# An 8 KB copy from DRAM to DRAM on a second DMA queue, issued at the start of an elementwise multiply-GELU kernel

**Chip, cores, metric.** One core of one Trainium2 chip. The metric is device time in microseconds (us), the median of several executions.

## The reference

```python
x, y: (1024, 4096) float32
z = x * y
out = 0.5 * z * (1 + tanh(sqrt(2 / pi) * (z + 0.044715 * z**3)))   # float32
```

Two inputs of 16.8 MB are read and one output of 16.8 MB is written, 50.33 MB in all, with two elementwise passes between.

## The kernel before

Each of the 128 partitions owns one contiguous stretch of 32768 floats of x, y and the output. SP is the sequencer of SyncE and ACT that of ScalarE; what a queue has for one of the 16 DMA engines is called its ring there. All transfers are issued by SP, so all sit on one queue: x in two halves, y in a half and two quarters, the output in two halves. VectorE multiplies in place and ScalarE applies GELU in place, in tiles of 4096 floats per partition.

```python
X_LOADS = [(0, 16384), (16384, 32768)]
Y_LOADS = [(0, 16384, 0), (16384, 24576, 0), (24576, 32768, 8192)]
STEP = 4096
STORES = [(0, 16384), (16384, 32768)]
# ...
    _hoist(nc, [load_x(0).ins, load_y(0).ins])   # placed ahead of SP's first drain, before the opening barrier
    load_x(1)
    for i in (1, 2):
        nc.sync.wait_ge(sem_mul, (Y_LOADS[i][1] - Y_LOADS[1][0]) // STEP)
        load_y(i)
# ... VectorE multiplies, ScalarE applies GELU, in tiles of STEP ...
    for i, (a, b) in enumerate(STORES):
        nc.sync.wait_ge(sem_act, b // STEP)
        nc.sync.dma_start(out=out_r[:, a:b], in_=xs[:, a:b]).then_inc(sem_o[i], 16)
```

Of the kernel before, what the change touches and what calls it, by code (L numbers as in the profile page):

```python
# [1 line left out]

# [4 lines left out]


F32 = mybir.dt.float32
GELU = mybir.ActivationFunctionType.Gelu_apprx_tanh  # L10
# [7 lines that stand above are left out]
Y_RING = 16384  # L18


def _hoist(nc, issued):

    here = nc.cur_bb.bb.instructions
    first = nc.main_func.blocks[0].instructions
    for ins in issued:
        del here[next(k for k, i in enumerate(here) if i is ins or i.name == ins.name)]
    engine = issued[0].engine
    at = next(
        k
        for k, i in enumerate(first)  # L30
        if i.engine == engine and type(i).__name__ == "InstDrain"
    )
    first[at:at] = issued


@with_exitstack
def kernel(
    ctx: ExitStack,
    tc: tile.TileContext,
    x: bass.AP,  # L40
    y: bass.AP,
    out: bass.AP,
):
    nc = tc.nc
    P = nc.NUM_PARTITIONS

    x_r = x.flatten_outer_dims().rearrange("(p a) c -> p (a c)", p=P)
    y_r = y.flatten_outer_dims().rearrange("(p a) c -> p (a c)", p=P)
    out_r = out.flatten_outer_dims().rearrange("(p a) c -> p (a c)", p=P)
    total_f = x_r.shape[1]  # L50


    tc.close()
    tc.compile()  # L54

    xs = nc.alloc_sbuf_tensor("xs", [P, total_f], F32).ap()
    ys = nc.alloc_sbuf_tensor("ys", [P, Y_RING], F32).ap()
    sem_x = [nc.alloc_semaphore(f"sem_x{i}") for i in range(len(X_LOADS))]
    sem_y = [nc.alloc_semaphore(f"sem_y{i}") for i in range(len(Y_LOADS))]
    sem_o = [nc.alloc_semaphore(f"sem_o{i}") for i in range(len(STORES))]  # L60
    sem_mul = nc.alloc_semaphore("sem_mul")
    sem_act = nc.alloc_semaphore("sem_act")

    def load_x(i):
        a, b = X_LOADS[i]
        return nc.sync.dma_start(out=xs[:, a:b], in_=x_r[:, a:b]).then_inc(sem_x[i], 16)  # L66

    def load_y(i):
        a, b, r = Y_LOADS[i]
        return nc.sync.dma_start(  # L70
            out=ys[:, r : r + b - a], in_=y_r[:, a:b]
        ).then_inc(sem_y[i], 16)

    _hoist(nc, [load_x(0).ins, load_y(0).ins])
    load_x(1)
    for i in (1, 2):
        nc.sync.wait_ge(sem_mul, (Y_LOADS[i][1] - Y_LOADS[1][0]) // STEP)
        load_y(i)

    n = 0  # L80
    for i, (a, b, r) in enumerate(Y_LOADS):
        for j, (xa, xb) in enumerate(X_LOADS):
            if xa <= a < xb:
                nc.vector.wait_ge(sem_x[j], 16)
        nc.vector.wait_ge(sem_y[i], 16)  # L85
        for c in range(a, b, STEP):
            nc.vector.tensor_mul(  # L87
                out=xs[:, c : c + STEP],
                in0=xs[:, c : c + STEP],
                in1=ys[:, r + c - a : r + c - a + STEP],  # L90
            ).then_inc(sem_mul, 1)
            n += 1
            nc.scalar.wait_ge(sem_mul, n)
            nc.scalar.activation(  # L94
                out=xs[:, c : c + STEP], in_=xs[:, c : c + STEP], func=GELU
            ).then_inc(sem_act, 1)

    for i, (a, b) in enumerate(STORES):
        nc.sync.wait_ge(sem_act, b // STEP)
        nc.sync.dma_start(out=out_r[:, a:b], in_=xs[:, a:b]).then_inc(sem_o[i], 16)  # L100
    for i in range(len(STORES)):
        nc.sync.wait_ge(sem_o[i], 16)
    nums = sorted(s.num for s in [*sem_x, *sem_y, *sem_o, sem_mul, sem_act])
    assert nums == list(range(nums[0], nums[-1] + 1))
    nc.sync.sem_clear(range(nums[0], nums[-1] + 1))


# [1 line left out]
_INS = ['x', 'y']  # L109
_OUTS = [((1024, 4096), 'float32')]  # L110


# [23 lines left out]
```

## Time and profile before

| | before |
|---|---|
| median time, 4 runs | 120.81 us (120.68 to 120.92) |
| span in the profile | 119.5 us |
| VectorE, ScalarE busy | 29%, 25% |
| DMA engines busy | 98.5% |
| rate over the span | 421 GB/s |

How to read it: the kernel moves data, and the compute engines wait. The end comes when the last of the 16 DMA engines has written its last row. Each transfer of 128 partition rows is split so that every engine gets 8 rows, and the trace has a record of each row. What a change can win or lose is in the few microseconds at the start, at the turn from loads to stores, and in any packet added. The prediction adds this up and shows the lines.

### The profile page before, as it was taken

The numbers are of one execution on the slowest core, as the hardware profiler recorded it, in microseconds if no ns is written. First come the engines' busy times: TensorE is split into PE (matmuls) and PEld (weight loads), VectorE is DVE, ScalarE is ACT, GpSimd is POOL, SyncE is SP. The second block draws the span as 40 slices with busy tenths as digits, with TensorE's granted clock in tenths as the row PEclk, the third lists the DMA queues.
The fourth block names the chain that finished last, engine by engine and source line by source line (L and its number), as shares of the span: only waits on it lengthen the run. The fifth ranks groups of instructions, "written<-read, shape, count | busy, mean of one in ns | idle before, by whom it ended". The sixth has DMA issues, their size and how long they took to land.

```text
span 119.5 us, 68 instructions
## 1 busy us (share of the span) xinstructions
DVE 35.0 (29%) x8; ACT 30.2 (25%) x9; POOL 0.2 (0%) x4
## 2 busy tenths in 40 slices
DVE  0000000000000199999600049959990000000000
ACT  3000000000000006797780000977479200000000
POOL 0000000000000000000000000000000000000000
DMA  9889888998899889988898989998899888988890
GB/s 351 351 373 680 351 351 351 636 417 351 351 636 417 351 351 526 526 351 351 351 526 351 504 373 482 395 526 351 351 395 658 351 351 351 702 351 351 351 680 22
DMA packets 1008, 50.33 MB, mean 421 GB/s; under 512 B 112, under 2 KB 112, under 8 KB 112
## 3 DMA queue, kind: packets, MB, share of 16 engines
q1 hardware_dynamic: 1008, 50.33, 98.5%
HBM read 33.55 MB, written 16.78 MB: 421 GB/s over the span
## 4 chain that ended last, share of the span: by engine, by line
DMA 53%; DVE 22%; ACT 3%; SPq 0%; issue 0%; DVEq 0%
DMA ys<-in_y_dram 53%; DVE xs L87 22%; ACT xs L94 3%; SPq L66 0%; DVEq L85 0%
## 5 line engine op out<-in xcount | busy, mean ns | idle before, releaser
L87 DVE TENSOR_TENSOR xs<-xs,ys 128x4096 f32<-128x4096 f32 x8 | 35.0, 4421 | 54.7 <-DMA ys<-in_y_dram 54.7
L94 ACT ACTIVATE xs<-xs 128x4096 f32<-128x4096 f32 x8 | 28.9, 3617 | 61.1 <-DVE xs L87 61.1
L94 ACT ACT_TABLE_LOAD x1 | 1.3, 1283 | 1.9 <-PEq L54 1.9
L120 POOL MEMSET const-bfloat16-1.0<- 128x1 bf16 x1 | 0.1, 102 | 0.0
L120 POOL MEMSET const-uint8-127<- 128x1 uint8 x1 | 0.1, 102 | 0.0
L120 POOL MEMSET const-float32-1.0<- 128x1 f32 x1 | 0.1, 99 | 0.0
L120 POOL MEMSET const-float32-0.0<- 128x1 f32 x1 | 0.1, 98 | 0.2 <-issue 0.2
## 6 DMA issues: line engine op xcount, KB each, us to landing
ys<-in_y_dram SPq DMA_DIRECT2D x2, 4096.0 KB, 21.1
xs<-in_x_dram SPq DMA_DIRECT2D x2, 40.3
out_dram<-xs SPq DMA_DIRECT2D x2, 31.9
ys<-in_y_dram SPq DMA_DIRECT2D x1, 40.8
```

The lines of the kernel that those rows point to most:

```text
L87: nc.vector.tensor_mul(out=xs[:, c : c + STEP], in0=xs[:, c : c + STEP], in1=ys[:, r + c - a : r + c - a + STEP],).then_inc(sem_mul, 1)
L94: nc.scalar.activation(out=xs[:, c : c + STEP], in_=xs[:, c : c + STEP], func=GELU).then_inc(sem_act, 1)
L120: nc = _bacc.Bacc("TRN2", target_bir_lowering=False, num_devices=1)
```

## The change

The intent, as the short description has it, is a first transfer on ACT's queue: 64 B per partition are copied from x to the head of each partition's stretch of the output, which the first store overwrites later. Why one would want it isn't stated; the likely hope is that a tiny transfer takes a start-up cost off the large one. To keep the result right, SP waits for its semaphore ahead of the first store.

```diff
+    sem_w = nc.alloc_semaphore("sem_w")
@@
+    first = nc.scalar.dma_start(out=out_r[:, :16], in_=x_r[:, :16])
+    first.then_inc(sem_w, 16)
+    _hoist(nc, [first.ins])
     _hoist(nc, [load_x(0).ins, load_y(0).ins])
@@
+    nc.sync.wait_ge(sem_w, 16)
     for i, (a, b) in enumerate(STORES):
@@
-    nums = sorted(s.num for s in [*sem_x, *sem_y, *sem_o, sem_mul, sem_act])
+    nums = sorted(s.num for s in [*sem_x, *sem_y, *sem_o, sem_w, sem_mul, sem_act])
```

## The prediction

> **What bounds the kernel now.** I read four views, from coarse to fine. First the top of the page: which engine is busy, and how full the DMA engines are.
>
> ```profile
> DVE 35.0 (29%) x8; ACT 30.2 (25%) x9; POOL 0.2 (0%) x4
> ...
> DMA  9889888998899889988898989998899888988890
> ...
> DMA packets 1008, 50.33 MB, mean 421 GB/s; under 512 B 112, under 2 KB 112, under 8 KB 112
> ...
> q1 hardware_dynamic: 1008, 50.33, 98.5%
> ```
>
> The reader is to see that no compute engine is busy a third of the span, while the 16 DMA engines have work for 98.5% of it, without a hole in the row of digits. All transfers sit on one queue. The 1008 packets are 7 transfers x 16 engines x (8 rows + 1 semaphore write).
>
> Second, the chain that ended last, in order of time:
>
> ```profile
> 0.00 0.39 SPq L66
> 0.39 0.05 issue
> 0.44 40.80 DMA ys<-in_y_dram
> ...
> 58.80 21.99 DMA ys<-in_y_dram
> ...
> 80.88 8.77 DVE xs L87 x2
> 89.66 0.02 issue
> 89.68 3.62 ACT xs L94
> ```
>
> It passes through the loads and the last multiply and GELU, and stops there: the last store, issued at 93.3, isn't in it. It mustn't be read as "22% DVE on the path". The waits of the DMA queue's issuer and the issue table say what the end is:
>
> ```profile
> SPq L102 <- DMA out_dram<-xs: 25.8, 1, 25.8
> ...
> out_dram<-xs SPq DMA_DIRECT2D x2, 31.9
> ```
>
> The issuer waits 25.8 us for the last store, and that store is slow to land because the first store is still in front of it on the same engines (the two took 37.7 and 26.1 us from issue to landing). So the end is set by how much the 16 engines have to move in all and by when they start, not by any issue time in between.
>
> Third, the busy time in stretches (a packet is booked in the stretch where it starts; columns are stretch, length, DVE, ACT, POOL, clock, DMA share, GB/s):
>
> ```profile
> 0.00:1.00 1.00, 0.00 (x0) 0.00 (x0) 0.20 (x4) 1.00 0.00 0
> 1.00:2.00 1.00, 0.00 (x0) 0.07 (x1) 0.00 (x0) 1.00 3.13 1049
> 2.00:4.00 2.00, 0.00 (x0) 1.21 (x1) 0.00 (x0) 1.00 0.00 0
> 4.00:6.00 2.00, 0.00 (x0) 0.00 (x0) 0.00 (x0) 1.00 1.21 524
> 6.00:59.00 53.00, 17.43 (x4) 11.05 (x4) 0.00 (x0) 1.00 1.01 435
> ```
>
> Nothing moves in the first microsecond. Between 1 and 2 us every engine starts its first 64 KiB row, and the share of 3.13 in a stretch of 1 us says that these rows take 3.13 us each. The next rows start between 4 and 6 us: 2 x 1.21 = 2.42 us each. So the first row of each engine is 0.71 us longer than a later one. That is the start-up cost that this change might aim at.
>
> The single DMA packet records of the trace bear it out: a 64 KiB row takes 2.418 us in steady state and 2.63 to 3.29 us as an engine's first; first packets start at 1.01 to 1.70 us; the engines end at 118.60 to 119.07 us. From them the whole time adds up. Each engine moves 50.33 MB / 16 = 48 rows of 64 KiB, 48 x 2.418 = 116.06. The last engine to finish starts at 1.68, adds 0.55 in its first row and 0.74 in two rows of 32 KiB near 77 us, where loads give way to stores; some tenths of small stretches and overlaps take it to 119.07. The semaphore's way to the issuer and the last clear take it to 119.5. The measured 120.78 lies 1.25 above that span, and I carry this difference over.
>
> **What the Trainium skill says.** "DMA: Bandwidth & Descriptors", Queues, rings and completion order: SP and ACT each have a ring of their own on each of the same 16 engines, and an engine goes round-robin between its rings at packet granularity. The trace before has one queue alone, so it can neither agree nor disagree; this is what puts the new rows in among the first rows of x and y. Same page, Bandwidth, Measured: a transfer of 4 KB has a floor that amounts to about 10.5 ns a packet (measured there on the gpsimd path, 64 packets). The trace has only semaphore writes of 4 B to compare, which take 9 ns, so of that order. Same page, Specifications: below 512 B an engine does read-modify-write; no transfer in this trace is so small, only semaphore writes. "Perfetto Trace Analysis", DMA Instruction — HWDGE: the descriptor generator is shared by the issuing sequencers and locked by one at a time. In the trace one issue occupies the sequencer 0.33 to 0.43 us; two issuers don't occur in it.
>
> **The change part by part.** It removes nothing.
>
> 1. One issue on ACT, hoisted ahead of the opening barrier. ACT's records in the trace start 0.13 us after SP's first issue, so the two come together, and the new transfer isn't really first. SP's first issue takes 0.39 us; if the generator is locked, ACT's goes in between SP's first and second, which delays the load of y by some 0.4 us. That load's rows queue behind 8 rows of x on each engine (8 x 2.42 = 19.4 us), so this costs nothing. If ACT instead got the lock first, all of x would start up to 0.4 us later and the end would move by that; I give this a fifth.
>
> 2. The opening barrier. ACT's drain comes some 0.4 us later, at about 0.55, but SP's comes after its second issue at 0.87, so SP still closes the barrier. The table load (1.93 to 3.21) has until 45.8, where the first GELU starts. Cost 0.
>
> 3. The data: 128 rows of 64 B, DRAM to DRAM, so 8 rows and one semaphore write for each engine. In bytes 8 KB, 0.02 us at 421 GB/s. In packets, with 9 to 10.5 ns for each of 9, about 0.09 us; if read-modify-write and the change from SBUF to DRAM as the target make one cost 60 ns (my guess, no row shows it), 0.5 us. I take 0.3 us. As the engines have no idle time, this is on the path in full.
>
> 4. The start-up of 0.71 us in the first rows. If it is an engine's first read from cold, whichever transfer comes first pays it. But a tiny row issued at the same moment can't pay it in advance: x's data would have to wait for the same first reads. The data of x in effect begins to flow at the end of the first row less 2.42 us, which is 1.6 to 2.2 us on all engines, whether they start at 1.01 or 1.70. For this to become earlier, the small rows would have to precede it clearly. I take 0.1 us of gain.
>
> 5. The wait for the new semaphore ahead of the stores: it is met some 40 us before the issuer comes to it, and the issuer is ahead of GELU there anyway. Cost 0. The clear at the end is still one instruction, over one more semaphore: 0.
>
> Sum: 0 + 0 + 0.3 - 0.1 + 0 = +0.2 us, so **121.0 us**.
>
> **The rivals.** (a) Warm-up works: the small transfer takes the 0.71 us off x's first rows, and perhaps some of the empty first microsecond. For it: the first rows really are longer than the others. Against: the two issues are 0.13 us apart. It would give 120.1 to 120.6. (b) Each alternation between the two rings empties the engine's pipeline: 8 alternations at a part of the 0.71 us, say 0.2 to 0.5, would be 1.6 to 4 us, and 122.4 to 124.8. For it: [...]at the one change of direction that the trace has, near 77 us, a row of 32 KiB is some 0.6 us longer. Against: 9-ns semaphore writes pass between long rows without a gap, and the next row's start overlaps the end of the one before by 3 ns, so reads run ahead. (c) The generator's lock goes to ACT first: +0.4, about 121.2. (d) All hidden: an engine waits for x's first data till about 1.9 us anyway and does the small rows in that hole: 120.8. Big gains are ruled out: 2% is 2.4 us, and the start (1.0), the first row (0.7) and the turn near 77 (0.7) together are as much as all that isn't pure data rate.
>
> **Range and chances.** Between (d) and the additive sum I put 70%, on rival (a) 9%, on (c) 13%, on (b) 8%. The runs before spread over 120.68 to 120.92. That gives 120.4 to 121.9 for 8 in 10. Faster by over 2% needs under 118.4, which the rate of the engines doesn't allow: 0.01. Slower by over 2% needs over 123.2, the larger half of (b): 0.05.
>
> **What would show it.** Right: a second queue with 144 packets and a share under half a per cent; the 2.42 us of a later row unchanged; the first rows near 3.1 us; SP's third issue late by at most 0.4 us; the last store's landing as long after its issue as before. Step 4 is wrong if x's first rows take about 2.4 us and the engines end earlier than 118.60 to 119.07. Step 3 is wrong if packets of 64 B show more than 60 ns each, or if there are gaps between x's rows in the first 20 us. Step 1 is wrong if x's first row starts later than 1.01 to 1.70 us after SP's first instruction, or if ACT runs clearly ahead of SP. What would overturn the prediction as a whole is a change of the 2.42 us with two rings in use, of which I see no sign in a trace with one ring.

## The result

| | before | changed |
|---|---|---|
| median time, 4 runs each | 120.81 us | 121.13 us (120.95 to 121.17) |
| ratio, 95% interval | | 1.0024 (1.0006 to 1.0041) |
| span in the profile | 119.5 us | 119.8 us |

The time is the same within 2%, and 0.3 us above before.

From the changed kernel's page:

```profile
DMA packets 1152, 50.34 MB, mean 420 GB/s; under 512 B 256, under 2 KB 256, under 8 KB 256
...
q1 hardware_dynamic: 1008, 50.33, 98.3%
q10 hardware_dynamic: 144, 0.01, 0.1%
```

The large queue is as it was, and a second one has 144 packets: 128 rows of 64 B and 16 semaphore writes, a tenth of a per cent of the engines' time.

The start of both timelines (start, duration, engine, line, operation), before and then changed:

```profile
0.44 0.43 SPq L70 DMA_DIRECT2D ys<-in_y_dram  x1
1.93 0.33 SPq L66 DMA_DIRECT2D xs<-in_x_dram  x1
```

```profile
0.00 0.39 SPq L67 DMA_DIRECT2D xs<-in_x_dram  x1
0.12 0.62 ACTq L75 DMA_DIRECT2D out_dram<-in_x_dram  x1
...
0.43 0.42 SPq L71 DMA_DIRECT2D ys<-in_y_dram  x1
2.08 0.33 SPq L67 DMA_DIRECT2D xs<-in_x_dram  x1
```

ACT comes 0.12 us after SP, so the "first" transfer isn't first. Its issue takes 0.62 us and overlaps both of SP's, which are not longer for it. The opening barrier ends 0.15 us later, seen in SP's third issue.

The stretches of the changed kernel (stretch, length, VectorE, ScalarE, GpSimd, clock, DMA share, GB/s):

```profile
1.00:2.00 1.00, 0.00 (x0) 0.00 (x0) 0.00 (x0) 1.00 3.13 1049
...
4.00:6.00 2.00, 0.00 (x0) 0.00 (x0) 0.00 (x0) 1.00 1.21 524
```

x's first rows still take 3.13 us each and the next ones 2.42. No start-up cost has gone. The issue table and the waits of the DMA issuer, changed kernel (issues: KB, us from issue to landing; waits: total, times, longest):

```profile
out_dram<-in_x_dram ACTq DMA_DIRECT2D x1, 8.0 KB, 24.2
```

```profile
SPq L105 <- ACT xs L98: 30.7, 1, 30.7
SPq L107 <- DMA out_dram<-xs: 25.8, 1, 25.8
SPq L104 <- ACT xs L98: 3.3, 1, 3.3
```

An 8 KB transfer takes 24.2 us to land. The row records say why: the engines take one 64 B row from ACT's ring, then one 64 KiB row from SP's, and so on eight times, and the first 64 B row comes at 6.49 us, after two long rows. SP comes to the first store (L104) and waits 3.3 us for GELU, so the new wait ahead of it had been met. The last store lands 25.8 us after SP begins to wait for it, as before.

**Where 0.3 us went in the first two profiles.** From the row records, as means over the 16 engines (the kept records carry no engine number; the rows of one engine are pieced together by their times, and the means don't depend on that):

| part | before | changed | difference |
|---|---|---|---|
| start of x's first row | 1.214 | 1.195 | -0.02 |
| length of x's first row | 3.128 | 3.130 | 0.00 |
| small excesses of later 64 KiB rows over 2.418 | 0.183 | 0.011 | -0.17 |
| 8 small rows and a semaphore write | none | 0.065 | +0.07 |
| excess of the 32 KiB rows over 1.213 (nearly all in the last two of each engine, called the hold below) | 0.705 | 0.842 | +0.14 |
| mean end of the engines | 118.784 | 118.783 | 0.00 |
| end of the last engine | 119.070 | 119.376 | +0.31 |

The 0.065 is worked out from the start-to-start time of consecutive 64 KiB rows: most often 2.414 us with nothing between them and 2.421 us with a small row between, so 8 x 7 ns + 9 ns. The mean end is the same in both, and the first engine even ends earlier (118.38 against 118.60); what is 0.3 us later is the last engine, which by this piecing together was held 1.35 us in the last two rows of y. Two theories follow. **A:** the transfer costs each engine 0.07 us, and the rest is scatter, which a single pair of profiles can't average out. **B:** the transfer really costs 0.3 us, by way of a longer turn from loads to stores. The experiments are to tell these apart, and to try the rivals from the prediction.

### The profile page after: what moved, and what is told of

Same layout as the page of the kernel before. It is cut to its first block, busy times and chain, and to the rows that moved or that the text cites. A ratio compares the mean times of both kernels' runs of the same rounds, so it can differ in the third digit from the quotient of the medians.

```text
span 119.8 us, 70 instructions
## 1 busy us (share of the span) xinstructions
DVE 35.0 (29%) x8; ACT 30.2 (25%) x9; POOL 0.2 (0%) x4
## 4 chain that ended last, share of the span: by engine, by line
DMA 53%; DVE 22%; ACT 3%; SPq 0%; issue 0%; DVEq 0%
DMA ys<-in_y_dram 53%; DVE xs L91 22%; ACT xs L98 3%; SPq L67 0%; DVEq L89 0%
## 6 DMA issues: line engine op xcount, KB each, us to landing
out_dram<-in_x_dram ACTq DMA_DIRECT2D x1, 8.0 KB, 24.2
```

## The experiments

Each ran beside the kernel before on the same chip. "Long row" is one of 64 KiB.

### c1_after_again and e1_after_third: the changed kernel again

No edit.

> The changed kernel once more, unaltered. The packet records of the first profile put only about 0.07 us of the change on each engine (8 rows of 64 B at 7 ns net, one semaphore write of 9 ns); the mean end of the 16 engines is the same in both profiles (118.78 us), only the last engine is 0.3 us later. Theory A (0.07 us is real, the rest is the luck of which engine is held longest where loads turn to stores): 5 rounds give a ratio of 1.000 to 1.0015. Theory B (the small transfer really costs about 0.3 us, by way of a longer turn): ratio 1.002 to 1.003 again, and the last engine again ends later than 119.2 us in the profile. Rival C (warm-up of the first rows): x's first rows would have to be under 3 us in the mean; the first profile has 3.13, as before, so they should be 3.1 again.

Measured: 121.17 us median against 121.02; ratio 1.0011 (0.9999 to 1.0023). The last engine ended at 119.51 us. x's first rows took 3.09 us in the mean. Warm-up is refuted once more; A and B both had some support, so a third set was run.

> The changed kernel a third time, on whichever chip this is, to narrow the size. The start-to-start time of consecutive 64 KiB rows in the profiles is 2.414 us before and 2.421 us with a small row between, so 8 x 7 ns = 0.06 us and 9 ns for the semaphore. Theory A (0.07 us and the rest scatter of the turn at 77 us): ratio 0.9995 to 1.0015. Theory B (0.3 us each time): 1.002 to 1.003. The second set of rounds gave 1.0011, between the two; the first 1.0024.

Measured: 121.00 against 120.90; ratio 1.0006 (0.9993 to 1.0019), last engine at 119.33. The three sets give 1.0024, 1.0011 and 1.0006. Weighted by their precision this is 1.0012, give or take 0.0008, or 0.14 us. The 0.07 us of the rows is a ratio of 1.0006, which lies in all three intervals (at the edge of the first). B's 1.002 to 1.003 lies above both later results, though the interval of c1 reaches into its low end and that of e1 stops just short of it. A last engine later than 119.2 us, which B expected, was seen twice, but the next run shows that in the kernel before too.

### c2_before_again: the kernel before against itself

No edit.

> The kernel before against itself, as a null control. All theories: ratio 1.000 within 0.1%. Its profile tells how much the turn near 77 us (0.70 us in the mean of the engines, 0.54 to 0.83) and the end of the last engine (119.07 us) scatter from one execution to the next. Theory A: they scatter by some 0.3 us. Theory B: the same to 0.1 us, with every engine held 0.6 to 0.8 us in the next-to-last row of y as before.

Measured: 120.96 against 121.02; ratio 0.9996 (0.9985 to 1.0008). Its profiled execution was a long one, 121.38 us, and its last engine ended at 119.60, later than in any profile of the changed kernel. The turn, in the first profile of before and then in this one:

```profile
76.50:78.00 1.50, 1.50 (x1) 1.50 (x1) 0.00 (x0) 1.00 1.21 350
```

```profile
76.50:78.00 1.50, 1.50 (x1) 1.50 (x1) 0.00 (x0) 1.00 1.53 350
```

A stretch with 350 GB/s over 1.5 us has 16 rows of 32 KiB, one on each engine. A share of 1.21 over 1.5 us makes 1.82 us for each, 1.53 makes 2.30 us, where a free one takes 1.213. With both last rows counted from the row records, the hold is 0.70 us in the one profile and 1.16 in the other (1.22 with all 32 KiB rows), from the same program. So the scatter that theory A needs is there without the change: 0.4 us in the mean end of the engines (118.78 and 119.19), and 0.5 us at the last engine. The chip of the first profile isn't on record, but the eleven runs of the kernel before that ran beside c2 on its chip spread over 0.61 us as well.

### c3_no_hoist: the small transfer after the opening barrier

```diff
-    _hoist(nc, [first.ins])
```

> The small transfer issued by ACT after the opening barrier, so that neither ACT's drain nor the barrier is in its way. If the change's cost comes from the 0.15 us later barrier or from ACT's drain (rival D), it goes back to the time before: ratio 1.000. If it comes from the rows on the engines (theories A and B), it stays at that of c1_after_again, the small rows start one or two long rows of x later, and the opening barrier ends at 1.93 us again instead of 2.08.

Measured: 121.10 against 121.02; ratio 1.0005 (0.9993 to 1.0017). SP's third issue is back at 1.91 us, so the 0.15 us came from ACT's issue in front of the barrier. The interval can't tell 1.000 from c1's 1.0011, so for a cost of this size the run is inconclusive about the barrier. One expectation missed: the small rows were to start later, yet the first came at 6.45 us, in the same place as before, although ACT issued at 1.92 instead of 0.12. The engines didn't turn to the second ring until about the end of their second long row in either case.

### c4_sbuf_dest: the same rows into SBUF, no wait ahead of the stores

```diff
-    first = nc.scalar.dma_start(out=out_r[:, :16], in_=x_r[:, :16])
+    scratch = nc.alloc_sbuf_tensor("scratch", [P, 16], F32).ap()
+    first = nc.scalar.dma_start(out=scratch, in_=x_r[:, :16])
@@
-    nc.sync.wait_ge(sem_w, 16)          # moved behind the stores
```

> The same 128 rows of 64 B from x, but into SBUF, and no wait ahead of the stores (the wait stands at the end). If the cost lies in the write of 64 B to DRAM or in the wait of the stores (rival E), the ratio falls to 1.000. If it is that of 8 more packets in the ring (theory A), 0.07 us as before and the packet records of 64 B again take about 11 ns. By theory B in the form 'DRAM writes upset the turn to stores', nothing of the 0.3 us is left.

Measured: 120.99 against 121.02; ratio 0.9995 (0.9983 to 1.0007). In the row records a small row into SBUF costs what one into DRAM does: 11 ns each, and 2.421 us from one long row to the next. So the write of 64 B to DRAM isn't dear, and the direct part of the cost doesn't come from it. The whole time is at 1.000, within its interval also at A's 1.0006, and below that of the changed kernel by about as much as the sets scatter; it can't decide between A and B's form with DRAM writes. Two more things show in its profile. ACT's issue is short:

```profile
0.13 0.37 ACTq L76 DMA_DIRECT2D scratch<-in_x_dram  x1
```

It takes 0.37 us in place of 0.62, and SP's third issue is at 1.91 us, as in the kernel before. So the longer issue, and with it the 0.15 us at the barrier, goes with the copy from DRAM to DRAM and not with a small transfer as such. And the first small rows come from 3.99 us on, after one long row and not after two; why, no run shows.

### d1_wait_alone: one more wait, no transfer

```diff
+    nc.sync.wait_ge(sem_x[0], 16)
     for i, (a, b) in enumerate(STORES):
```

> The kernel before with one more wait ahead of the stores, on a semaphore that has long been reached (x's first load), and no small transfer. Rival E (the wait costs something): some of the 0.3 us. Theories A and B: 1.000, as the issuer comes to this wait some 3 us ahead of the GELU that it has to wait for anyway.

Measured: 121.00 against 121.01; ratio 1.0001 (0.9988 to 1.0015). The wait costs nothing that shows.

### d2_sp_first: the small transfer on SP's queue, ahead of x

```diff
-    first = nc.scalar.dma_start(out=out_r[:, :16], in_=x_r[:, :16])
+    first = nc.sync.dma_start(out=out_r[:, :16], in_=x_r[:, :16])
```

> The small transfer on SP's own queue, ahead of x's first load, so that it really is first on each engine's ring. Start-up theory 1 (the first row of an engine is long since the engine is cold, and the small row takes that on itself): x's first rows fall from 3.13 to about 2.4 us; they start 0.43 us later (one more issue), so the whole is 0.2 to 0.3 us faster than before, ratio 0.998. Start-up theory 2 (the 0.71 us is the time that a long row's own first data takes, whatever went before): x's first rows stay near 3.1 us and the whole is later by the issue, 0.4 us and 0.07 for the packets: ratio 1.004.

Measured: 121.79 against 121.01; ratio 1.0064 (1.0049 to 1.0079). The start of its timeline:

```profile
0.00 0.64 SPq L75 DMA_DIRECT2D out_dram<-in_x_dram  x1
...
0.69 0.57 SPq L67 DMA_DIRECT2D xs<-in_x_dram  x1
```

Now the small transfer is first, and it lands 2.3 us after its issue. x's first rows still take 3.21 us in the mean, and they start at 2.12 us instead of 1.21. Start-up theory 1 falls. The direction of theory 2 was right, the size was too small: the issue in front takes 0.69 us, not 0.43, and x's own issue takes 0.57 instead of 0.39.

### d3_gate: x waits until the small transfer has landed

```diff
-    _hoist(nc, [load_x(0).ins, load_y(0).ins])
+    gate = nc.sync.wait_ge(sem_w, 16)
+    _hoist(nc, [gate.ins, load_x(0).ins, load_y(0).ins])
@@
-    nc.sync.wait_ge(sem_w, 16)          # ahead of the stores; the gate replaces it
```

> The small transfer on ACT, and SP waits until it has landed before it issues x. A full warm-up, whatever it costs. The landing of a lone small transfer should take about 2 us from its issue, so the end moves later by some 2 us: 122.5 to 123.2. What counts is x's first rows in the profile: 2.4 us (cold start, theory 1) or about 3.1 us (their own first read, theory 2), and whether the gap from SP's issue to the first row falls below 1.0 us.

Measured: 123.40 against 121.01; ratio 1.0201 (1.0186 to 1.0216), a little above the expected range and, against the 2% line, unclear. Timeline and stretches:

```profile
0.01 0.60 ACTq L75 DMA_DIRECT2D out_dram<-in_x_dram  x1
...
2.21 0.38 SPq L67 DMA_DIRECT2D xs<-in_x_dram  x1
```

```profile
2.00:4.00 2.00, 0.00 (x0) 0.00 (x0) 0.00 (x0) 1.00 1.56 524
```

This is as full a warm-up as this small transfer can give: every engine has moved eight rows and written its semaphore before x is issued. x's 16 first rows all start in this stretch and take 2 x 1.56 = 3.12 us each, the same as in the kernel before. They start 3.33 - 2.21 = 1.12 us after x's issue, against 1.21 before. So the longer first row isn't the cold start of an engine, and this small transfer doesn't remove it. One might say that the engines went cold again in the 1.70 us between the small transfer's semaphore writes and x's rows (means); in d2_sp_first that pause is 0.45 us, and x's first rows took 3.21 us.

### e3_x_split: smaller first rows, no small transfer

```diff
-X_LOADS = [(0, 16384), (16384, 32768)]
+X_LOADS = [(0, 4096), (4096, 16384), (16384, 32768)]   # both pieces go to _hoist ahead of y; VectorE's waits to match
```

> The kernel before, without a small transfer, with x's first load cut in two: 16 KiB rows, then 48 KiB rows. It asks what the 0.71 us of each engine's first row is, as a small row ahead of it did not take it away. If it grows with the size of the first row (the 16 engines' first burst), a 16 KiB first row is some 0.2 us longer than 0.60 us, and the end is up to 0.5 us earlier: ratio 0.996. If it is the time of the first data whatever the row (theory 2), the first row takes 1.3 us in place of 0.60, nothing is gained, and the extra issue and 9-ns semaphore write cost nothing visible: ratio 1.000.

Measured: 120.93 against 120.90; ratio 1.0001 (0.9986 to 1.0017). The 16 KiB first rows took 1.165 us in the mean, against 0.61 for a later one: 0.55 us of excess, where the 64 KiB row has 0.71. Most of it doesn't shrink with the row, and the end doesn't move. This fits theory 2 better than growth with the size (which was to leave 0.2 us), though some 0.1 us of the excess is not in these rows, nor in the second ones (0.05 us).

### d4_rows4 and e2_rows_4k: more rows, larger rows

```diff
+    out_k = out_r.rearrange("p (k c) -> p k c", c=4096)
+    x_k = x_r.rearrange("p (k c) -> p k c", c=4096)
-    first = nc.scalar.dma_start(out=out_r[:, :16], in_=x_r[:, :16])
+    first = nc.scalar.dma_start(out=out_k[:, :4, :16], in_=x_k[:, :4, :16])
```

> Four times as many small rows: 512 of 64 B, 32 on each engine. By the packet records of the change (7 ns net for each, one after each long row of SP's ring) this adds 32 x 7 = 0.22 us on each engine plus the semaphore, so 0.23 us in the mean end of the engines against 0.07 with the change. Round-robin one packet for one packet means that the small rows go on for 32 long rows, so the transfer lands at about 70 us after its issue, and the first store waits for it (62.4 before), which costs nothing as its turn on the engines comes only near 79 us. If instead a small row costs 60 ns, the end moves by 1.9 us.

Measured: 121.04 against 121.01; ratio 1.0027 (0.9993 to 1.0062), drawn up by one run of 122.49; the other five lie between 120.97 and 121.28. The time can't resolve 0.22 us here. The records bear the mechanism out: the step from long row to long row is 2.421 us up to 55 us, and the issue table shows how long 32 turns take:

```profile
out_dram<-in_x_dram ACTq DMA_DIRECT2D x1, 32.0 KB, 68.9
```

A guess of 60 ns per small row (1.9 us) is ruled out by the median. To see the cost above the scatter, the rows have to be larger:

```diff
-    first = nc.scalar.dma_start(out=out_r[:, :16], in_=x_r[:, :16])
+    first = nc.scalar.dma_start(out=out_r[:, :1024], in_=x_r[:, :1024])
```

> The same transfer with 4096 B per partition in place of 64 B, still 8 rows on each engine and one issue on ACT. If what a row in the second ring costs is the engine's time for it (theory A, by bytes): 4096 B at 65536 B in 2.414 us is 0.15 us a row, 8 rows 1.21 us, and all of it at the end, since the engines have no idle time: ratio 1.010, x's row-to-row time 2.57 us in the first 20 us. If it is hidden anyway (rival: the engines have slack), the ratio stays at 1.001. If rows from DRAM to DRAM cost double, 1.020.

Measured: 122.01 against 120.90; ratio 1.0090 (1.0076 to 1.0103). The queues in its page:

```profile
q1 hardware_dynamic: 1008, 50.33, 97.6%
q10 hardware_dynamic: 144, 0.52, 1.1%
```

The second queue's share is 1.1%, and the whole is 0.9% longer. The step between long rows is 2.569 us, so a 4 KiB row costs 0.155 us, 1.24 us for eight. The engines have no slack: what the second ring takes comes out at the end. From DRAM to DRAM costs one row's time, not two.

### f1_late_store: what the turn is

```diff
         nc.sync.wait_ge(sem_act, b // STEP)
+        nc.sync.wait_ge(sem_y[2], 16)
```

> The kernel before, with the first store held back until y's last load has landed, so that no store is queued behind the last two 32 KiB rows of y. It asks whether what holds the engines there (0.70 us in the mean in the first profile of before, 1.22 in the second, 0.84 to 1.17 with the change) belongs to the turn from loads to stores. If so, the excess of the 32 KiB rows over 1.213 us falls under 0.1 us, at the price of idle engines from the landing to the first store's packets: some 2 to 3 us, ratio 1.015 to 1.025. If it comes from something else at that time (VectorE and ScalarE at work on SBUF, a rival), the excess of 0.7 to 1.2 us stays.

Measured: 121.63 against 120.95; ratio 1.0058 (1.0037 to 1.0080), where 1.015 to 1.025 was expected. The stretch shown for c2 and the ones after it, in this run:

```profile
76.50:78.00 1.50, 1.50 (x1) 1.50 (x1) 0.00 (x0) 1.00 0.83 350
78.00:79.50 1.50, 1.34 (x1) 0.78 (x2) 0.00 (x0) 1.00 0.81 350
79.50:81.00 1.50, 0.59 (x1) 1.50 (x1) 0.00 (x0) 1.00 0.00 0
81.00:82.00 1.00, 1.00 (x1) 1.00 (x1) 0.00 (x0) 1.00 2.46 1049
```

0.81 x 1.5 = 1.22 us: y's last rows run free although VectorE and ScalarE are as busy as ever, and then the engines stand idle. By the row records the hold is 0.03 us in the mean. (Over all 32 KiB rows the excess is 0.22 us, above the 0.1 expected; 0.19 of it lies in rows ahead of the last two.) The hold in the last rows belongs to the store queued behind them. The price was mis-sized: the idle time is 1.70 us on an engine in the mean, but the hold that is saved gives back 0.4 to 1.2 of it. The last line shows one thing more: the store's first rows, after this pause, take 2.46 us each, 0.04 more than the steady 2.418. The 0.71 us of x's first rows is not what any row after a pause costs.

No version beats the kernel before: every variant is at 1.000 within its interval or slower. None of the experiments points to a faster one.

## Why the prediction was right, and where its terms were off

The forecast of 121.0 us held: 121.13 in the first rounds, 121.17 and 121.00 in the later ones. Step by step:

1. **The issue on ACT.** Right that the two come together (0.12 us apart) and that x isn't delayed (first rows at 1.20 us in the mean, 1.21 before). No wait for the generator's lock shows: SP's second issue began at 0.43, as before, while ACT's was under way. ACT's issue takes 0.60 to 0.62 us, not 0.4. It takes 0.60 alone too (d3_gate), and SP needs 0.64 for the same transfer (d2_sp_first), so this is the transfer's own (0.37 for the same rows into SBUF, c4_sbuf_dest), not a wait for a lock. By the prediction's own sign the step would count as wrong, as one engine's first row started at 1.94 us, later than 1.70; but f1_late_store, without a small transfer, has one at 1.91, so the sign, drawn from one profile, was too narrow.
2. **The barrier.** It ends 0.15 us later, where the prediction had SP closing it as before: with ACT's issue behind the barrier (c3_no_hoist) or short (c4_sbuf_dest) the 0.15 us is gone. A cost for the whole isn't visible (c3_no_hoist), though nothing below 0.1% is resolved.
3. **The rows.** Right in kind (they alternate with x's and are paid in full, as e2_rows_4k shows for rows of 4 KiB), off in size: 0.3 us was taken, 0.065 measured. The lower figure in that step, 0.09 us from 9 to 10.5 ns a packet, was nearly right; the guess of up to 60 ns was wrong.
4. **The first rows' 0.71 us.** Right that the small transfer can't take it away; the 0.1 us of gain was still too much, 3.13 us is unchanged. The reason given, that the small rows would have to come clearly ahead, was wrong: in d3_gate they do, and nothing is gained.
5. **The new wait.** 0, right (d1_wait_alone).

The sum of the measured terms is thus +0.07 us where the prediction had +0.2. The measured differences of the means are 0.29, 0.10 and 0.09 us. That the forecast fell on the first result so closely owes something to scatter: c2_before_again shows that the last engine's end moves by 0.5 us between executions of one program. In that pair of profiles it is mostly the turn, where the hold differs by 0.46 us and the mean end by 0.41. But the turn isn't the only source: in d1_wait_alone the hold was 0.45 us while earlier 32 KiB rows lost 0.55, and f1_late_store, without a hold, still spread over 0.53 us in four runs.

What stays open is whether up to some 0.17 us beyond the rows' own 0.07 belong to the change (the three sets give 0.14 give or take 0.10), by way of the turn. The five profiles with 8 rows of 64 B issued on ACT beside x have holds of 0.84 to 1.16 us, the four without a small transfer and with the first store as it was (before, c2, d1, e3) 0.45 to 1.16. The ranges overlap: the runs neither show nor exclude it.

Of the rivals, (a) warm-up is refuted. (b), a pipeline that empties at each alternation, is refuted by the 7 ns. (c), ACT ahead of SP, didn't occur. (d), all hidden in the hole at the start, is refuted as a mechanism: the small rows don't run there, but from 6.5 us on. (Rival (c) has a fifth in step 1 and 13% among the chances; it can't have both. And that the last engine to finish starts at 1.68 us can't be checked, since the kept records have no engine number.)

## What to carry to other kernels

In these runs, where the DMA engines are busy throughout, a small transfer on a second queue cost about the engine time of its rows (measured for rows of 4 KiB; for 64 B the total is too small to see), and its time to land was set by the long rows that it alternates with: 8 KB took 24 us. Before adding a warm-up, check whether the first row's excess is the engine's cold start at all: let a tiny transfer land before the first large one and read the first row's length. And judge a difference of 0.3% from several sets of rounds and several profiles, since the profile of a single execution showed the same program 0.5 us apart.

## What the Trainium skill lacked or had wrong

- "DMA: Bandwidth & Descriptors", Queues, rings and completion order: round-robin between rings agrees with the row records. It speaks of typically 9 to 17 descriptors in a packet; here the turn passed after a single row, 64 B of the one ring against 64 KiB of the other, so that 8 rows took eight turns and 8 KB landed after 24.2 us (32 rows: 68.9 us). It lacks when the second ring gets its first turn: for the copy from DRAM to DRAM only after two long rows, from about 6.4 us on, whether issued at 0.12 or 1.92 us, and for the same rows into SBUF after one, from 3.99 us on.
- "DMA: Bandwidth & Descriptors", Specifications: the warning about transfers under 512 B holds as to the rate: a 64 B row cost an engine 7 ns net, where 64 B at the pace of the long rows (65536 B in 2.414 us) would take 2.4 ns. The penalty is thus some 5 ns a row, the same to DRAM as to SBUF; whether read-modify-write is behind it, no run shows.
- "Perfetto Trace Analysis", DMA Instruction — HWDGE: no wait for a generator locked by one sequencer at a time shows: ACT's issue (0.12 to 0.74 us) overlapped two of SP's without lengthening them (0.39 and 0.42 us, before 0.39 and 0.43), and took 0.60 us alone. A lock held for a small part of an issue isn't excluded. The page lacks that a copy of 8 KB from DRAM to DRAM took 0.60 to 0.64 us to issue, the same rows into SBUF 0.37 us, and a load of 8 MB 0.33 to 0.43 us.
- On no page: the engines are held 0.4 to 1.2 us in the mean in their last loads when a store is queued behind them (0.03 us when none is), and this varies between profiles of one program (0.70 and 1.16 us).
- No page says whether an engine's earlier work shortens the first row of a load. Here the first row of x was longer than later ones by 0.55 us (16 KiB) to 0.71 us (64 KiB), and stayed so when the engine had just moved small rows (0.70 and 0.79 us in d3_gate and d2_sp_first); a store's first row after 1.70 us without work was longer by 0.04 us only (f1_late_store).
